# A chain of three transformer blocks on one core: four instead of three blocks of columns taken by halves of the tokens at a change of stage, their low parts made on DVE instead of POOL

## The chip, the core and the metric

The kernel runs on one core of a Trainium2 chip. The core has a matrix engine (PE, with its weight loads PEld), a vector engine (DVE), an activation engine (ACT), a general engine (POOL) and a queue engine that issues loads (SP). The metric is the time of one execution in microseconds on the device; lower is better.

## The reference

512 tokens of width 1024 go through three blocks, all in float32. What matters here is where a new activation meets its first weights:

```
x = layer_norm(DN_ALPHA * x + 0.5 * swiglu_ffn(x, ffn1_wg, ffn1_wu, ffn1_wd), ...)      # ffn1
y = parallel_mixers(x, w_in, ...)     # h @ w_in: qkv, z, gates, glu; gated delta rule, conv branch
x = layer_norm(DN_ALPHA * x + y, ...)
x = layer_norm(DN_ALPHA * x + memory_cross_attention(x, mem, w_xq, ...), ...)           # x @ w_xq
x = layer_norm(DN_ALPHA * x + 0.5 * swiglu_ffn(x, ffn2_wg, ffn2_wu, ffn2_wd), ...)      # ffn2
x = second_block(x, ...)              # retention and sparse attention
x = third_block(x, ...)               # neighbourhood and latent attention, then a SwiGLU (ffn3)
```

`swiglu_ffn` is `(silu(x @ w_gate) * (x @ w_up)) @ w_down`. In `parallel_mixers` the product with `w_in` gives, per head, the queries, keys and values of a chunked gated delta rule (GDN), the gates of its decay, and the two halves of a gated linear unit (GLU) for a 31-tap convolution.

## The kernel before

**Products.** A float32 product is made of three matmuls in a reduced type: every operand is split into a high part and a low part (`mm3`, lines 210 to 214). A weight block is loaded by `wload` (line 349): SP loads 128 x 1024 values to a raw buffer `wr` (2 buffers), ACT casts them to the high part `wh` (line 346; 4 buffers), and an engine that the caller names subtracts to get the low part `wl` (line 347; 4 buffers). That engine is DVE, except in the GDN stage (`now["lo"] = G`), and where the caller passes POOL (`G`).

**Changes of stage.** A stage ends in `block_out` (line 474): the last products of the four rows of 128 tokens are consumed one row after another. Each row goes through a chain on DVE: add the residual (line 493), statistics (509, 376), the reciprocal root (line 370, with a power on POOL, line 371), two instructions of line 381 and two of line 382, which scale and shift the two halves of the row. Each half is then turned by four PE transposes (line 364) and split on ACT and DVE (lines 346 and 347, `x<-mm`), which makes the new activation.

**By halves.** The next stage needs all four rows for a matmul over 512 tokens, but only rows one and two for one over the first 256. So at the start of ffn1, GDN, cross-attention, ffn2 and ffn3 the function `by_halves` (line 409) loads some blocks of 128 columns, takes all of them over the first half of the tokens, and then all of them over the second: 24 matmuls of 256 columns per block and half. Before, these are three blocks: gate, gate and up in the three ffn (a fourth block, the second up, follows over 512 tokens), key, query and value of head 0 in GDN, three blocks of queries in cross-attention. The low parts are made by POOL, except in ffn1's start, where three blocks were loaded early with DVE (`early`).

**What sets the order.** The code is written as generators; a scheduler places each engine's instructions in one order by its own estimate of times, within the dependences. Each engine runs its own order and waits where an operand is not there. In the GDN stage the order of emission is kept (`keep_order`): a list of units (24 matmuls of a block, line 294) fills PE between the steps of the chains (`procs`), and DVE is filled with convolution taps (line 654). There, the PSUM banks are shared out by `banks(pj=3, tp=1, gt=3, cv=1)`.

Of the kernel before, what the change touches and what calls it, by code (L numbers as in the profile page):

```python
# [108 lines left out]
def kernel(ctx: ExitStack, tc: tile.TileContext, a: dict, out: bass.AP, upto=99):  # L109
# [299 lines left out]
    def by_halves(jobs, act):  # L409


        ws = []
        for src, c0, banks in jobs:
            n = len(banks)
            ws.append(early.pop(0) if early else
                      [wload(src, k0, 8 // n, c0, n * 128, G) for k0 in range(0, 8, 8 // n)])
        for hf in range(2):
            ts_ = slice(hf * 256, (hf + 1) * 256)
            for (src, c0, banks), w in zip(jobs, ws):
                n = len(banks)  # L420
                for i in range(n):
                    cs = slice(i * 128, (i + 1) * 128)
                    for k in range(8):
                        h, l = w[k // (8 // n)]
                        mm3(banks[i][:, ts_], (h[:, k % (8 // n), cs], l[:, k % (8 // n), cs]),
                            (act.hi(k)[:, ts_], act.lo(k)[:, ts_]), k == 0, k == 7)
                yield
# [112 lines left out]
    def swiglu(act, wg, gc, wu, uc, scale, h, f0, f1, first=None):  # L540

        wg, wu = dram_w(wg), dram_w(wu)
        for fp in range(f0, f1, 2):
            ps = []
            if fp == f0 == first:
                ps = [[bank(), bank()], [bank(), bank()]]
                yield from by_halves([(w, c0 + (fp + f) * 128, [ps[i][f]])
                                      for i, f, w, c0 in ((0, 0, wg, gc), (0, 1, wg, gc), (1, 0, wu, uc))], act)
                wh, wl = wload(wu, 0, 8, uc + (fp + 1) * 128, 128)
                for k in range(8):  # L550
                    mm3(ps[1][1], (wh[:, k], wl[:, k]), (act.hi(k), act.lo(k)), k == 0, k == 7)
                yield
            for w, c0 in ((wg, gc), (wu, uc)) if not ps else ():
                pp = [bank(), bank()]
                ps.append(pp)
                for kh in range(2):
                    hi, lo = wload(w, 4 * kh, 4, c0 + fp * 128, 256)
                    for f in range(2):
                        cs = slice(f * 128, (f + 1) * 128)
                        for k in range(4):  # L560
                            mm3(pp[f], (hi[:, k, cs], lo[:, k, cs]), (act.hi(4 * kh + k), act.lo(4 * kh + k)),
                                kh == 0 and k == 0, kh == 1 and k == 3)
                    yield
            for f in range(2):
                sg = t2()
                A.activation(sg, ps[0][f], AF.Silu)  # L566
                V.scalar_tensor_tensor(sg, sg, scale, ps[1][f], OP.mult, OP.mult)  # L567
                split(sg, h.hi(fp + f), h.lo(fp + f), G)
            yield
# [65 lines left out]
    cv = {}  # L635

    def glu_conv(c):
        w = dram_w("w_in")
        act = acts["b1_1"]
        ps = []  # L640

        def taps(o):
            s_ = []

            def first():
                pad = work("pad", (128, T + 30))
                G.memset(pad[:, :30], 0.0)
                A.copy(pad[:, 30:], o)
                s_.extend((pad, bank(tag="cv")))
                A.activation(s_[1], pad[:, 0:T], AF.Identity, bias=cols["convb"][:, c:c + 1], scale=tap31(0, c))  # L650

            def tap(j):
                pad, p = s_
                V.scalar_tensor_tensor(p if j < 30 else o, pad[:, j:j + T], tap31(j, c), p, OP.mult, OP.add)  # L654

            background[1].append(first)
            background[1].extend([lambda j=j: tap(j) for j in range(1, 31)])

        def consume():
            if c % 2 == 0:  # L660
                cv.setdefault("out", []).append(slot(FT, tag="ma"))
            o = cv["out"][c // 2][:, c % 2]
            A.copy(o, ps[0])
            sg = work("xr", (128, T))
            A.activation(sg, ps[1], AF.Sigmoid)
            yield 1500.0
            G.tensor_tensor(o, o, sg, OP.mult)
            yield 1500.0
            taps(o)

        def body(h, l):
            p = bank()
            for k in range(8):
                mm3(p, (h[:, k], l[:, k]), (act.hi(k), act.lo(k)), k == 0, k == 7)
                yield 1
            ps.append(p)
            if len(ps) == 2:
                spawn(consume())

        unit((w, 0, 8, 4112 + c * 128, 128), body)  # L680
        unit((w, 0, 8, 4112 + 1024 + c * 128, 128), body)

    def conv_norm():
# [36 lines left out]
    gd = {}  # L720
# [79 lines left out]

    def gdn_start():
        ps = {i: bank() for i in (1, 0, 2)}
        gd["pre", 0] = ps
        yield from by_halves([(dram_w("w_in"), i * 1024, [ps[i]]) for i in (1, 0, 2)], acts["b1_1"])

    def gdn_rows(h):

# [411 lines left out]
    def cross_queries():  # L1219
        w = dram_w("w_xq")  # L1220
        act = acts["b1_2"]
        qt = xa["q"] = Act(slot)

        def consume(f, p):
            A.activation(qt.hi(f), p, AF.Copy, scale=1.0 / 16)
            V.scalar_tensor_tensor(qt.lo(f), p, 1.0 / 16, qt.hi(f).bitcast(FT), OP.mult, OP.subtract)

        ps = [bank() for _ in range(3)]
        yield from by_halves([(w, f * 128, [ps[f]]) for f in range(3)], act)
        for f in range(3):  # L1230
            consume(f, ps[f])
        yield from feature_proj(w, 384, 5, act, 8, lambda f, p: consume(f + 3, p))

    def cross_attention():
        qt = xa["q"]
# [761 lines left out]
    with ExitStack() as outer:  # L1997
        outer.enter_context(room(dict(ma=12)))
        mark("gdn")
        with room(vk=6, mt=4, at=4, Y=4, X=2, pad=2, xr=3, sq=1, t2=4, sqc=1, gsmall=1, ub=1, yb=1, tb=1):  # L2000
            sq, lev = t2((128, 3, 128)), work("sqc", (128, 2, 128))
            S.dma_start(sq, a["k_squares"][:, 1:4])
            for i, j in enumerate((2, 4)):
                S.dma_start(lev[:, i], a["k_squares"][:, j])
            triu, ones, gneg, lev = sq[:, 0], sq[:, 2], lev[:, 0], lev[:, 1:2]
            zero = work("sq", (128, 4, 128))
            V.memset(zero, 0.0)
            for t in ("sm", "sy", "sx"):
                gd[t] = dpool.tile([64, BLOCK_STEP], FT, name=t)
            for t in ("sy", "sx"):  # L2010
                for i in range(2):
                    S.dma_start(chunks(gd[t], i), zero)
            now["lo"] = G
            run(gdn_start())
            banks(pj=3, tp=1, gt=3, cv=1)
            gdn_rows(0)
            gdn_gates()
            spawn(gdn_pair(0))
            for what in (glu_conv, 0), (gdn_rows, 1), (glu_conv, 1), (gdn_rows, 2), (gdn_rows, 3), (glu_conv, 2), \
                    (gdn_rows, 4), (glu_conv, 3), (gdn_rows, 5), (gdn_z, 0), (gdn_z, 1), (glu_conv, 4), (gdn_rows, 6), \  # L2020
                    (gdn_rows, 7), (glu_conv, 5), (gdn_z, 2), (gdn_z, 3), (glu_conv, 6), (gdn_z, 4), (gdn_z, 5), \
                    (glu_conv, 7), (gdn_z, 6), (gdn_z, 7), *[(gdn_gate, f) for f in range(8)]:
                what[0](what[1])
            split_ahead(2)
            while True:
                fill_dve()
                start = len(nc.cur_bb.bb.instructions)
                if not step():
                    break
                keep_order(start)  # L2030
            for left in background[1]:
                left()
            now["lo"] = V
        wide()
        mark("mix2")
        with room(dict(m=10), mf=6, t2=5):
            run(gate_proj("gcx", "w_in", 7184, acts["b1_1"], None, "mf"))
            run(split_o())
            run(interleave((gated("ga", "w_gdn_out", gd["oact"], 8, None), 1.0), (seq(conv_norm(), conv_act()), 0.5)))
            run(merge("y1", "ga", "gcx", "w_conv_out", cv["act"], 8, cols["bco"], "ma"))  # L2040
            mark("mixout")
            run(block_out(acts["y1"], 8, dram_w("w_mix_out"), residual(x_dram["b1_1"], "mf"), ALPHA, ("ln2_g", "ln2_b"),
                          "b1_2", out if upto == 2 else None, tag="mf"))
# [126 lines left out]
```

## Time and profile before

| what | value |
|---|---|
| median of three runs | 2798.34 us (2793.07 to 2801.97) |
| profiled execution, its own time | 2799.25 us |
| its span, first to last instruction | 2797.5 us |
| mean granted clock of PE | 0.983 |
| PE busy | 2673.2 us (96%) |
| DVE busy | 1375.7 us (49%) |
| ACT busy | 1065.4 us (38%) |
| POOL busy | 477.5 us (17%) |

Busy shares are means over stages. PE's matmuls are pipelined, so that matmuls recorded with 0.28 us may follow each other every 0.12 us; the distance of their starts tells what one costs.

### The profile page before, as it was taken

How to read it: one execution, taken by the hardware profiler on the slowest of the kernel's cores; microseconds unless marked ns; L12 is line 12 of the kernel's file. 1: busy time of each engine (PE TensorE's matmuls, PEld its weight loads, DVE VectorE, ACT ScalarE, POOL GpSimd, SP SyncE). 2: the span in 40 equal slices, each digit the busy share in tenths (PEclk: the TensorE clock that was granted, in tenths of full speed). 3: DMA queues.
4: the chain of work that ended last, by engine and by line, in shares of the span. 5: the costliest groups of instructions: out<-in, count | busy, mean ns of one | idle time of the engine just before them, and what ended most of it. 6: DMA issues, size and time to landing. Idle time of an engine off the chain costs nothing. (4 is left out here: it accounts for less than half of the span.)

```text
span 2797.5 us, 34810 instructions
## 1 busy us (share of the span) xinstructions
PE 2673.2 (96%) x13600; PEld 2170.6 (78%) x13600; DVE 1375.7 (49%) x2459; ACT 1065.4 (38%) x2000; POOL 477.5 (17%) x357
## 2 busy tenths in 40 slices
PE   9999999897898899999999989999999999999998
PEld 7888877776677688888888867775786767888887
DVE  3232357665568556453332365674455464622324
ACT  3222236554543332433212254563255464332221
POOL 0101035343331011001101030131002001211011
PEclk9999999998999999999999999999999999999999
DMA  6323356556555234524333334312235122433332
GB/s 193 97 95 95 97 118 86 86 77 94 61 72 91 83 124 125 173 76 158 98 97 94 97 101 125 98 43 80 91 98 92 56 59 95 159 112 98 95 94 83
DMA packets 330421, 277.30 MB, mean 99 GB/s; under 512 B 50360, under 2 KB 282513, under 8 KB 330257
## 3 DMA queue, kind: packets, MB, share of 16 engines
q1 hardware_dynamic: 292768, 251.20, 35.3%
q10 hardware_dynamic: 37488, 23.88, 2.8%
q8 instruction: 107, 1.75, 0.3%
q14 instruction: 58, 0.47, 0.1%
HBM read 256.64 MB, written 20.49 MB: 99 GB/s over the span
## 5 line engine op out<-in xcount | busy, mean ns | idle before, releaser
L212 PE MATMUL mm<-x,wl 128*128 128x512 f32 (+3 forms) x2072 | 808.0, 390 | 8.9 <-POOL wl L347 5.9
L347 DVE TENSOR_TENSOR wl<-wr,wh 128x1024 fp32r<-128x1024 f32 (+1 forms) x351 | 429.4, 1224 | 784.5 <-ACT wh L346 783.3
L213 PE MATMUL mm<-x,wh 128*128 128x512 f32 (+3 forms) x2072 | 792.8, 383 | 0.0
L214 PE MATMUL mm<-x,wh 128*128 128x512 f32 (+3 forms) x2072 | 792.3, 382 | 0.0
L346 ACT CAST wh<-wr 128x1024 fp32r<-128x1024 f32 (+2 forms) x425 | 436.3, 1027 | 796.9 <-PE mm L214 523.9
L212 PEld LDWEIGHTS mm<-x,wl 128*128 128x128 f32 (+2 forms) x2072 | 395.1, 191 | 82.9 <-POOL wl L347 6.3
L214 PEld LDWEIGHTS mm<-x,wh 128*128 128x128 f32 (+2 forms) x2072 | 394.5, 190 | 75.9 <-issue 1.8
L213 PEld LDWEIGHTS mm<-x,wh 128*128 128x128 f32 (+2 forms) x2072 | 395.6, 191 | 68.4 <-issue 1.4
L347 POOL TENSOR_TENSOR wl<-wr,wh 128x1024 fp32r<-128x1024 f32 x74 | 177.0, 2394 | 543.9 <-ACT wh L346 521.6
L347 POOL TENSOR_TENSOR h<-t,h 128x512 fp32r<-128x512 f32 x66 | 101.6, 1539 | 837.0 <-ACT h L346 837.0
L214 PE MATMUL mm<-wh,h 128*128 128x512 f32 x528 | 205.6, 389 | 0.0
L212 PE MATMUL mm<-wh,h 128*128 128x512 f32 x528 | 205.6, 389 | 0.0
L213 PE MATMUL mm<-wl,h 128*128 128x512 f32 x528 | 205.6, 389 | 0.0
L654 DVE SCALAR_TENSOR_TENSOR mm<-pad,cols,mm 128x512 f32<-128x512 f32 x232 | 174.7, 753 | 27.4 <-ACT mm L650 21.8
L212 PEld LDWEIGHTS mm<-wh,h 128*128 128x128 f32 x528 | 99.1, 188 | 20.6
L214 PEld LDWEIGHTS mm<-wh,h 128*128 128x128 f32 x528 | 99.1, 188 | 20.5
L213 PEld LDWEIGHTS mm<-wl,h 128*128 128x128 f32 x528 | 99.1, 188 | 20.4
L566 ACT ACTIVATE t<-mm 128x512 f32<-128x512 f32 x66 | 39.4, 597 | 130.7 <-PE mm L214 130.7
L567 DVE SCALAR_TENSOR_TENSOR t<-t,mm 128x512 f32<-128x512 f32 x66 | 45.4, 687 | 78.1 <-POOL h L347 54.9
L212 PE MATMUL mm<-m,wl 128*128 128x512 f32 (+1 forms) x224 | 81.6, 364 | 0.0
L214 PE MATMUL mm<-m,wh 128*128 128x512 f32 (+1 forms) x224 | 81.3, 363 | 0.0
L213 PE MATMUL mm<-m,wh 128*128 128x512 f32 (+1 forms) x224 | 81.0, 362 | 0.0
(454 smaller groups left out, 3691.6 us busy)
## 6 DMA issues: line engine op xcount, KB each, us to landing
wr<-in_w_in SPq DMA_DIRECT2D x122, 512.0 KB
wr<-in_ffn_wg SPq DMA_DIRECT2D x44, 512.0 KB
wr<-in_ffn_wu SPq DMA_DIRECT2D x44, 512.0 KB
wr<-in_ffn_wd SPq DMA_DIRECT2D x44, 512.0 KB
wr<-in_w_ffn_in SPq DMA_DIRECT2D x44, 512.0 KB
wr<-in_w_ffn_out SPq DMA_DIRECT2D x22, 512.0 KB
xd<-m ACTq DMA_DIRECT2D x32, 256.0 KB
wr<-in_w_xkv SPq DMA_DIRECT2D x16, 512.0 KB
```

The lines of the kernel that those rows point to most:

```text
L212: PE.matmul(o, lh[1], rh[0], start=start, stop=False)
L213: PE.matmul(o, lh[0], rh[1], start=False, stop=False)
L214: PE.matmul(o, lh[0], rh[0], start=False, stop=stop)
L346: A.copy(hi, src)
L347: (eng or V).tensor_sub(lo, src, hi.bitcast(FT))
L566: A.activation(sg, ps[0][f], AF.Silu)
L567: V.scalar_tensor_tensor(sg, sg, scale, ps[1][f], OP.mult, OP.mult)
L654: V.scalar_tensor_tensor(p if j < 30 else o, pad[:, j:j + T], tap31(j, c), p, OP.mult, OP.add)
```

## The change

Four blocks go by halves instead of three. In the ffn stages the fourth is the second up block, which was taken over 512 tokens just behind. In cross-attention it is the fourth block of queries (of eight). In GDN it is the first block of the GLU's linear half, which was a unit of the stage before; its bank is taken from the tag `gt`, so that the banks are now shared out before `gdn_start` and not behind it, and `glu_conv(0)` finds that product ready. The low parts of all blocks that `by_halves` loads are made by DVE (`V`) instead of POOL (`G`).

```diff
@@ by_halves
             ws.append(early.pop(0) if early else
-                      [wload(src, k0, 8 // n, c0, n * 128, G) for k0 in range(0, 8, 8 // n)])
+                      [wload(src, k0, 8 // n, c0, n * 128, V) for k0 in range(0, 8, 8 // n)])
@@ swiglu
                 yield from by_halves([(w, c0 + (fp + f) * 128, [ps[i][f]])
-                                      for i, f, w, c0 in ((0, 0, wg, gc), (0, 1, wg, gc), (1, 0, wu, uc))], act)
-                wh, wl = wload(wu, 0, 8, uc + (fp + 1) * 128, 128)
-                for k in range(8):
-                    mm3(ps[1][1], (wh[:, k], wl[:, k]), (act.hi(k), act.lo(k)), k == 0, k == 7)
-                yield
+                                      for i, w, c0 in ((0, wg, gc), (1, wu, uc)) for f in range(2)], act)
@@ glu_conv
-        ps = []
+        ps = [gd["glu"]] if c == 0 else []
...
-        unit((w, 0, 8, 4112 + c * 128, 128), body)
+        if not ps:
+            unit((w, 0, 8, 4112 + c * 128, 128), body)
         unit((w, 0, 8, 4112 + 1024 + c * 128, 128), body)
@@ gdn_start
-        gd["pre", 0] = ps
-        yield from by_halves([(dram_w("w_in"), i * 1024, [ps[i]]) for i in (1, 0, 2)], acts["b1_1"])
+        gd["pre", 0], gd["glu"] = ps, bank(tag="gt")
+        yield from by_halves([(dram_w("w_in"), i * 1024, [ps[i]]) for i in (1, 0, 2)] +
+                             [(dram_w("w_in"), 4112, [gd["glu"]])], acts["b1_1"])
@@ cross_queries
-        ps = [bank() for _ in range(3)]
-        yield from by_halves([(w, f * 128, [ps[f]]) for f in range(3)], act)
-        for f in range(3):
+        ps = [bank() for _ in range(4)]
+        yield from by_halves([(w, f * 128, [ps[f]]) for f in range(4)], act)
+        for f in range(4):
             consume(f, ps[f])
-        yield from feature_proj(w, 384, 5, act, 8, lambda f, p: consume(f + 3, p))
+        yield from feature_proj(w, 512, 4, act, 8, lambda f, p: consume(f + 4, p))
@@ tile_decoder_kernel, the GDN stage
-            run(gdn_start())
             banks(pj=3, tp=1, gt=3, cv=1)
+            run(gdn_start())
```

DVE's order at the change from ffn1 to GDN, before, from the affine steps of the third row (`m_1098`) to the splits of the fourth row (`m_1100`):

```order
L381 SCALAR_TENSOR_TENSOR m_1098<-m_1098,mv_2527,m_2158 128x512 x2
L382 SCALAR_TENSOR_TENSOR m_1098<-m_1098,lr_2529,m_2160 128x512 x2
L493 SCALAR_TENSOR_TENSOR m_1100<-m_1100,mm_2331 128x512
L509 BN_STATS st_2326<-m_1100 128x6
L347 TENSOR_TENSOR x_2445<-mm_2535,x_2444 128x4x128
L376 BN_AGGR mv_2573<-st_2326 128x2
L347 TENSOR_TENSOR x_2457<-mm_2545,x_2456 128x4x128
L370 TENSOR_SCALAR lr_2575<-mv_2573 128x1
L381 SCALAR_TENSOR_TENSOR m_1100<-m_1100,mv_2573,m_2158 128x512 x2
L382 SCALAR_TENSOR_TENSOR m_1100<-m_1100,lr_2575,m_2160 128x512 x2
L347 TENSOR_TENSOR x_2445<-mm_2581,x_2444 128x4x128
L347 TENSOR_TENSOR x_2457<-mm_2591,x_2456 128x4x128
```

The same place after (the rows are `m_1122` and `m_1124` now):

```order
L382 SCALAR_TENSOR_TENSOR m_1122<-m_1122,lr_2553,m_2184 128x512 x2
L493 SCALAR_TENSOR_TENSOR m_1124<-m_1124,mm_2355 128x512
L347 TENSOR_TENSOR wl_2656<-wr_2654,wh_2655 128x1024
L347 TENSOR_TENSOR x_2469<-mm_2559,x_2468 128x4x128
L347 TENSOR_TENSOR x_2481<-mm_2569,x_2480 128x4x128
L509 BN_STATS st_2350<-m_1124 128x6
L347 TENSOR_TENSOR wl_2662<-wr_2660,wh_2661 128x1024
L376 BN_AGGR mv_2597<-st_2350 128x2
L370 TENSOR_SCALAR lr_2599<-mv_2597 128x1
L381 SCALAR_TENSOR_TENSOR m_1124<-m_1124,mv_2597,m_2182 128x512 x2
L382 SCALAR_TENSOR_TENSOR m_1124<-m_1124,lr_2599,m_2184 128x512 x2
L347 TENSOR_TENSOR wl_2668<-wr_2666,wh_2667 128x1024
```

The second, third and fourth blocks' subtractions (`wl`) now stand in DVE's order within the fourth row's chain; the first stands before line 493 of the first row. The other three changes of stage read alike, save that in them a fourth block's subtraction stood behind the last line 382 before, too.

PE's order at the same change of stage, before, where it meets the transposes of the fourth row (line 364), 43 half matmuls of 72 into the first half of the tokens:

```order
L214 MATMUL mm_2621<-x_2456,wh_2630 128x256
L212 MATMUL mm_2621<-x_2456,wl_2631 128x256
L364 MATMUL mm_2581<-ident,m_1100 128x128 x4
L213 MATMUL mm_2621<-x_2457,wh_2630 128x256
L214 MATMUL mm_2621<-x_2456,wh_2630 128x256
L364 MATMUL mm_2591<-ident,m_1100 128x128 x4
```

And after, 62 half matmuls of 96 into it:

```order
L212 MATMUL mm_2646<-x_2480,wl_2662 128x256
L213 MATMUL mm_2646<-x_2481,wh_2661 128x256
L364 MATMUL mm_2605<-ident,m_1124 128x128 x4
L214 MATMUL mm_2646<-x_2480,wh_2661 128x256
L212 MATMUL mm_2646<-x_2480,wl_2662 128x256
L364 MATMUL mm_2615<-ident,m_1124 128x128 x4
```

The transposes moved from the second block's first half (`mm_2621`) to the third's (`mm_2646`). Those of the third row stand after six and seven half matmuls in both.

## Rows read from the trace of the kernel before

**Rows 1.** Waits of PE: waiter, releaser, total us, times, longest.

```profile
PE mm L693 <- DVE ma L654: 12.3, 1, 12.3
...
PE mm L364 <- issue: 6.3, 4, 1.6
...
PE mm L364 <- DVE mf L382: 4.1, 2, 2.1
PE mm L364 <- DVE m L382: 4.1, 2, 2.1
```

**Rows 2.** Timeline, PE, into GDN: start, us, instruction, count, [idle before, releaser].

```profile
378.08 0.63 PE L364 MATMUL mm<-ident,m 128*128 128x128 f32 x4 [1.55 <-issue]
...
380.88 0.63 PE L364 MATMUL mm<-ident,m 128*128 128x128 f32 x4 [2.05 <-DVE m L382]
...
382.18 0.41 PE L212 MATMUL mm<-x,wl 128*128 128x256 f32 x1
382.39 0.41 PE L213 MATMUL mm<-x,wh 128*128 128x256 f32 x1
...
387.16 0.60 PE L364 MATMUL mm<-ident,m 128*128 128x128 f32 x4
387.51 0.36 PE L213 MATMUL mm<-x,wh 128*128 128x256 f32 x1
...
400.13 0.40 PE L212 MATMUL mm<-x,wl 128*16 128x512 f32 x1
```

**Rows 3.** Timeline, DVE, into GDN; the last row is from ffn2's start.

```profile
373.80 1.40 DVE L381 SCALAR_TENSOR_TENSOR m<-m,mv,m 128x512 f32<-128x512 f32 x2
375.12 5.62 DVE L382 SCALAR_TENSOR_TENSOR m<-m,lr,m 128x512 f32<-128x512 f32 x2
380.66 0.67 DVE L493 SCALAR_TENSOR_TENSOR m<-m,mm 128x512 f32<-128x512 f32 x1
...
384.62 1.41 DVE L382 SCALAR_TENSOR_TENSOR m<-m,lr,m 128x512 f32<-128x512 f32 x2
...
1268.65 1.22 DVE L347 TENSOR_TENSOR wl<-wr,wh 128x1024 fp32r<-128x1024 f32 x1
```

**Rows 4.** Timeline, POOL, into GDN.

```profile
373.96 0.98 POOL L371 TENSOR_TENSOR lr<-lr,nhalf 128x1 f32<-128x1 f32 x1 [4.30 <-DVE lr L370]
374.92 5.27 POOL L347 TENSOR_TENSOR wl<-wr,wh 128x1024 fp32r<-128x1024 f32 x2
```

**Rows 5.** Windows, PE: stretch, us, busy (count), granted clock, DMA share, GB/s.

```profile
375.66:400.13 24.47, 20.87 (x161) 0.93 0.64 149
1078.95:1106.01 27.06, 22.72 (x176) 0.94 0.51 157
1258.30:1283.80 25.50, 21.82 (x162) 0.87 0.65 222
2421.63:2445.88 24.25, 20.61 (x161) 0.93 0.69 233
```

**Rows 6.** Timeline, PE, ffn1: 24 half matmuls apart, then 24 full ones apart.

```profile
16.20 0.28 PE L214 MATMUL mm<-x,wh 128*128 128x256 f32 x1
...
19.08 0.28 PE L214 MATMUL mm<-x,wh 128*128 128x256 f32 x1
...
31.67 0.39 PE L213 MATMUL mm<-x,wh 128*128 128x512 f32 x1
...
37.12 0.39 PE L213 MATMUL mm<-x,wh 128*128 128x512 f32 x1
```

**Rows 7.** Timeline, ACT: a cast into GDN, and a fourth block's into ffn2.

```profile
374.55 1.06 ACT L346 CAST wh<-wr 128x1024 fp32r<-128x1024 f32 x1 [0.33 <-PE mm L214]
...
1265.20 1.05 ACT L346 CAST wh<-wr 128x1024 fp32r<-128x1024 f32 x1
```

**Rows 8.** Timeline, PE, GDN: the first joins of two pairs of heads.

```profile
506.12 1.16 PE L208 MATMUL mm<-X,mt 128*128 128x128 f32 x8 [1.32 <-DMA X<-sx]
...
580.59 2.11 PE L208 MATMUL mm<-X,mt 128*128 128x128 f32 x16 [1.42 <-DMA X<-sx]
```

**Rows 9.** Timeline, PE, cross-attention: transposes of the memory's second half.

```profile
1099.96 1.06 PE L1165 MATMUL mm<-ident,mf 128*128 128x128 f32 x8 [0.76 <-DMA mf<-in_mem]
```

More of the change, by code (lines that the diff above doesn't have):

```diff
@@ L2013 @@
             now["lo"] = G
+            banks(pj=3, tp=1, gt=3, cv=1)
             run(gdn_start())
-            banks(pj=3, tp=1, gt=3, cv=1)
             gdn_rows(0)
```

## The prediction

> **What bounds the kernel now.** I read the page first: PE is busy 96% of the span of 2797.5 us and every other engine half or less, so the time is PE's work plus the places where PE stands still. The view of who waited for whom, for PE, comes next [rows 1]. Its longest entry is one wait of 12.3 us on the vector engine, late in the GDN stage. For this change three other entries count: the transposes at line 364, by which a new activation enters a stage, waited 4 times on "issue" (6.3 us) and 4 times on the affine step of line 382 (4.1 + 4.1 us). That is twice at each of four changes of stage: into GDN, cross-attention, ffn2 and ffn3.
>
> The timeline of the first of them shows how [rows 2 to 4]. PE begins the half-token blocks at 375.66 us [rows 5]. After six matmuls it meets the two transposes of the third row of 128 tokens, and stands 1.55 and then 2.05 us, until 380.88. DVE is why: its two affine steps of that row, 1.41 us together for the fourth row at 384.62, take 5.62 us from 375.12 on [rows 3]. In just that time, from 374.92 for 5.27 us, POOL makes the low parts of two weight blocks [rows 4]; POOL's tiny power at 373.96 had not slowed the step at 373.80. So a large POOL subtraction holds back a DVE instruction that reads two SBUF tensors. After the two gaps PE's matmuls of 256 columns come 0.21 us apart (382.18 to 382.39) where they otherwise come 0.12 apart [rows 2, 6]; the granted clock of the four stretches is 0.87 to 0.94 [rows 5]. The gaps thus cost twice, as idle time and as matmuls at the 1.2 GHz level.
>
> **What the four places lose.** A block of 24 half matmuls takes 2.88 us (16.20 to 19.08), a group of four transposes adds 0.36 (387.16 to 387.51) [rows 2, 6]. Three blocks by two halves and the four groups of rows three and four then need 144 x 0.12 + 4 x 0.36 = 18.72 us. They take 24.47 (GDN), 25.50 (ffn2) and 24.25 (ffn3) [rows 5]: losses of 5.75, 6.78 and 5.53. Cross-attention has four more groups, of the memory's rows, so 20.16 of 27.18 (27.06 and the last matmul's own 0.12); less the 0.76 that these wait for their own load [rows 9] it loses 6.26.
>
> **The change part by part.** *DVE instead of POOL.* Per place three subtractions of some 2.6 us (two in 5.27) leave POOL and three of 1.22 (row at 1268.65 [rows 3]) join DVE, in its order: the first ahead of row one's chain, where DVE is idle and at GDN at worst 0.1 us late; the second behind the fourth row's first step (line 493); the third before its statistics are joined; the fourth block's, which was DVE's already except in GDN, behind its affine steps. With nothing from POOL beside them the third row's affine steps end at 376.5. PE gets to its transposes at 375.66 + 6 x 0.12 = 376.4, needs one half at that time (ready 375.9) and the other at 376.9: no wait. So both gaps go, and with them the slow clock.
>
> *What is late next.* Row four. Its chain on DVE ran from 380.66 to the end of line 382 at 386.03, 5.37 us. It now starts at 376.5 and has two subtractions in it: 376.5 + 5.4 + 2 x 1.2 = 384.3. The fourth block's subtraction ends at 385.5, the splits of the fourth row at 386.8. PE meets row four's transposes after 62 half matmuls of 96 (before: after 43 of 72), so at 375.66 + 62 x 0.12 + 2 x 0.36 = 383.8 for the first, whose half is ready at 383.6, and 384.4 for the second, ready at 384.3. That is a tie. The second block is needed at 379.3 (ready 378.3), the third at 382.2 (381.4), the fourth at 386.4 (385.5), the second half of the tokens at 389.1 (386.8). The casts that these subtractions wait for ran at 374.55 and, for a fourth block, at 1265.20, some 7 us into its place [rows 7]. Nothing waits by more than some tenths. *Four blocks* is what keeps it so: with three, row four's transposes would stand at 375.66 + 43 x 0.12 + 0.72 = 381.5, 2.8 us before their data.
>
> *Price of halves.* The fourth block took 24 matmuls of 512 columns, 5.45 us (31.67 to 37.12), and takes 2 x 2.88 [rows 6]: 0.31 more, at five places (ffn1's start too, where three low parts were DVE's already; its fourth load now stands among the small column loads on SP, some 1.5 us for those, which PE's column transposes have in hand).
>
> *Cross-attention.* The load of the memory's second half waits on SP for the write of row four, and PE waited 0.76 us for it [rows 9]. The write moves up by some 3 us and PE gets there some 3.5 sooner, so I put 0.5 against the gain.
>
> *GDN.* There the fourth block was not the next work: it is the first GLU block, and 5.45 us of PE filler leave the stage that follows. That stage is a chain: gates, decay, scores, a solve by way of DRAM, joins. PE waits for its loads at the joins (1.32 us at 506.12, 1.42 at 580.59 [rows 8]), so filler taken out before a join is partly paid back as a longer wait. The gates begin at 400.13 before [rows 2] and at 375.66 + 192 x 0.12 + 1.44 = 400.1 after: the chain starts no sooner. By the order 318 full matmuls instead of 336 stand between gates and first join, and 147 instead of 156 before the last scores: these come 9 x 0.227 = 2.0 us sooner, and the solve with them. From the second join on the order is as before, to the 12.3 us wait at the end, which keeps its taps. Bounds: 0 (the chain ignores PE) and 5.75 - 0.31 = 5.4 (PE's gain passes whole). I take 2.0, the scores' move.
>
> **A rule weighed.** Rows 3 and 4 show a POOL operation holding a DVE one. The Trainium skill, page "SBUF — State Buffer", section "SBUF: two separate sides", says that the two share a port pair as an exclusive lock, for a DVE operation with two SBUF inputs against a GpSimd one that reads SBUF, and that whichever starts first keeps it for its whole length. By that the new subtractions on DVE could in turn hold POOL's power step of the row's norm (line 371). The rows show that power running beside line 381, at 373.96, unharmed, and in the new order no subtraction stands between line 370 and line 382. By the rule it costs nothing here, unless the engines drift by a subtraction, which is rival two's price.
>
> **Sum.** GDN 2.0; cross-attention 6.26 - 0.31 - 0.5 = 5.4; ffn2 6.78 - 0.31 = 6.5; ffn3 5.53 - 0.31 = 5.2; ffn1 -0.3. Together 18.8. The profiled run took 2799.25 us (span 2797.5), 0.9 above the median of 2798.34, which is nothing. 2799.25 - 18.8 = 2780.5.
>
> **The rivals.** *One, GDN takes it back.* Filler leaves ahead of the first join and DVE, ACT and POOL orders shift up to the second; if the solve doesn't come sooner and a queue adds a wait like those of rows 8 at one or two joins, GDN ends 0 to 4 us later: 2780.5 + 2 + 0 to 4, about 2784 to 2787. For it: PE does wait at both joins. Against: the scores move up.
>
> *Two, DVE becomes late.* Row four is a tie, so if DVE's three subtractions cost one instruction more (1.2 us) PE stands at the transposes again, 1.2 us at each of four places, 4.9 together: 2785. If the gap also drops the clock, which it did behind gaps of 1.6 and 2.1 us and then cost about 1.7 (19 matmuls 0.09 us too far apart), 11.7: 2792. For it: no slack in the sum above. Against: two tenths of slack at the next steps, and a gap under those seen.
>
> *Three, slower than before.* DVE works in order, and the second subtraction stands ahead of both splits of the third row and of row four's statistics. Its cast (374.55, done 375.6) waits for a buffer that PE's last matmuls of the old stage free, and its raw weights for a load. If one came late, DVE's whole chain would stand behind it and PE behind the chain. To eat the gain at the three places outside GDN (17 us) and GDN's 2 it must be 4.7 us late at each place, so not before 381.8. The cast is 1.5 us ahead of its need: it decides only from 6 us later on; 2803 at 6 us.
>
> *Four, all of it passes.* GDN's 5.4 and no memory wait: 22.7, so 2776.5.
>
> **How the numbers follow.** Forecast with rival four (2774 to 2784): 0.66. Rival one 0.14, rival two 0.16, rival three 0.04. The range holds the forecast with the spread of the three runs (some 4 us either way) below rival four, and reaches up over rival one and the dearer part of rival two's first price: 2773 to 2791. About 0.3%, 8.4 us, is what a measurement of this kernel can tell from none: faster means below some 2790. All of the forecast, of rival one and half of rival two lie there, less a little for the spread: faster 0.85, same 0.11, slower 0.04.
>
> **What would show it.** Line 382 in no place above 0.8 us an instruction; no PE wait at line 364 but a few tenths; granted clock 1.0 in the four stretches; POOL without large subtractions there. Per place PE needs 192 x 0.12 + 1.44 = 24.5 us for four blocks (26 in cross-attention). In GDN the first join at about 504 us, with a PE wait of 2 to 4 us before it, and its end some 2 us sooner. Wrong it would be by a new wait at row four's transposes, by a low clock without a gap, or by a GDN stage that is longer than before.

## The result, and the profile after

The changed kernel takes 2774.56 us (median of four runs, 2771.17 to 2778.54) where the kernel before takes 2795.70 (four runs, 2792.01 to 2801.97). The ratio is 0.9923, 95% interval 0.9911 to 0.9935: 21.5 us less, between 18.2 and 24.9. Forecast were 2780.5 us, 18.8 less than the profiled run of before.

PE's waits in the changed kernel (waiter, releaser, total us, times, longest) no longer hold the three entries at line 364 on "issue" (a wait for which the profile shows no releaser) and on line 382 that [rows 1] show. One of 2.5 us on a low part of weights is new:

```profile
PE mm L690 <- DVE ma L650: 13.4, 1, 13.4
...
PE mm L364 <- DMA m<-in_x: 5.8, 2, 5.0
...
PE mm L212 <- DVE wl L347: 2.5, 1, 2.5
```

The stretches of [rows 5], now four blocks by two halves each, PE alone (stretch, us, busy, granted clock, DMA share, GB/s):

```profile
377.01:404.51 27.50, 25.02 (x209) 1.00 0.67 153
1071.47:1098.13 26.66, 26.66 (x225) 1.00 0.53 178
1244.73:1269.51 24.78, 24.78 (x210) 1.00 0.79 271
2401.51:2426.27 24.76, 24.76 (x209) 1.00 0.79 274
```

In three of the four PE is busy for the whole stretch, and the granted clock is 1.00 in all, where it was 0.87 to 0.94. DVE's timeline at GDN's start (start, us, instruction) answers to [rows 3]:

```profile
376.48 1.41 DVE L382 SCALAR_TENSOR_TENSOR m<-m,lr,m 128x512 f32<-128x512 f32 x2
...
378.41 1.22 DVE L347 TENSOR_TENSOR wl<-wr,wh 128x1024 fp32r<-128x1024 f32 x1
...
384.10 1.41 DVE L382 SCALAR_TENSOR_TENSOR m<-m,lr,m 128x512 f32<-128x512 f32 x2
388.75 1.23 DVE L347 TENSOR_TENSOR wl<-wr,wh 128x1024 fp32r<-128x1024 f32 x1 [3.24 <-ACT wh L346]
```

The third row's two steps of line 382 take 1.41 us where they took 5.62. The last row is the fourth block's low part, which DVE makes 3.24 us late. Behind it stand the cast and the load (ACT, then SP), and PE waits for it:

```profile
387.67 1.04 ACT L346 CAST wh<-wr 128x1024 fp32r<-128x1024 f32 x1 [8.16 <-DMA wr<-in_w_in]
```

```profile
379.65 0.37 SPq L353 DMA_DIRECT2D wr<-in_w_in  x1
```

```profile
390.03 0.38 PE L212 MATMUL mm<-x,wl 128*128 128x256 f32 x1 [2.48 <-DVE wl L347]
```

The load is issued at 379.65, just when the second block's subtraction (378.41, 1.22 us) is done: there are two raw buffers, and that subtraction frees the one that the fourth block needs. The data are there 8.0 us later.

Both traces by stretches, each from its first half-token matmul to the next one's:

| stretch | before | after | less | forecast |
|---|---|---|---|---|
| start, ffn1 | 375.66 | 377.01 | -1.35 | -0.3 |
| GDN to cross-attention | 703.29 | 694.46 | 8.83 | 2.0 |
| cross-attention to ffn2 | 179.35 | 173.26 | 6.09 | 5.4 |
| ffn2 to ffn3 | 1163.33 | 1156.78 | 6.55 | 6.5 |
| ffn3 to the end | 375.87 | 370.89 | 4.98 | 5.2 |
| span | 2797.5 | 2772.4 | 25.1 | 18.8 |

These two executions lie 25.1 us apart, the runs 21.5.

### The profile page after: what moved, and what is told of

It is laid out like the page before. It is cut to its first block, busy times and chain, and to the rows that moved or that the text cites. A ratio compares the mean times of both kernels' runs of the same rounds, so it can differ in the third digit from the quotient of the medians.

```text
span 2772.4 us, 35041 instructions
## 1 busy us (share of the span) xinstructions
PE 2670.9 (96%) x13720; PEld 2173.4 (78%) x13720; DVE 1370.9 (49%) x2472; ACT 1064.5 (38%) x1999; POOL 445.2 (16%) x344
## 5 line engine op out<-in xcount | busy, mean ns | idle before, releaser
L347 DVE TENSOR_TENSOR wl<-wr,wh 128x1024 fp32r<-128x1024 f32 (+3 forms) x364 | 444.5, 1221 | 801.1 <-ACT wh L346 799.7
L212 PE MATMUL mm<-x,wl 128*128 128x512 f32 (+1 forms) x2112 | 812.9, 385 | 10.7 <-POOL wl L347 5.9
L214 PE MATMUL mm<-x,wh 128*128 128x512 f32 (+1 forms) x2112 | 797.9, 378 | 0.0
L213 PE MATMUL mm<-x,wh 128*128 128x512 f32 (+1 forms) x2112 | 797.8, 378 | 0.0
L346 ACT CAST wh<-wr 128x1024 fp32r<-128x1024 f32 (+3 forms) x425 | 436.3, 1027 | 811.0 <-PE mm L214 502.7
L212 PEld LDWEIGHTS mm<-x,wl 128*128 128x128 f32 x2112 | 400.4, 190 | 83.1 <-POOL wl L347 6.3
L214 PEld LDWEIGHTS mm<-x,wh 128*128 128x128 f32 x2112 | 400.1, 189 | 74.3 <-issue 1.8
L213 PEld LDWEIGHTS mm<-x,wh 128*128 128x128 f32 x2112 | 401.0, 190 | 67.2 <-issue 1.4
L347 POOL TENSOR_TENSOR wl<-wr,wh 128x1024 fp32r<-128x1024 f32 (+1 forms) x61 | 144.2, 2364 | 297.3 <-ACT wh L346 279.1
L371 POOL TENSOR_TENSOR lr<-lr,nhalf 128x1 f32<-128x1 f32 x24 | 23.6, 984 | 371.3 <-DVE lr L370 371.3
L214 PE MATMUL mm<-m,wh 128*128 128x512 f32 (+1 forms) x224 | 81.2, 363 | 0.0
```

Of the source, the lines that this page charges most:

```text
L212: PE.matmul(o, lh[1], rh[0], start=start, stop=False)
L213: PE.matmul(o, lh[0], rh[1], start=False, stop=False)
L214: PE.matmul(o, lh[0], rh[0], start=False, stop=stop)
L346: A.copy(hi, src)
L347: (eng or V).tensor_sub(lo, src, hi.bitcast(FT))
L371: G.tensor_tensor(o, o, nhalf[:, :n], OP.pow)
```

## The experiments

Three questions: is it the engine or the fourth block that gains; what holds DVE while POOL works; and what is GDN's share, 2.0 or 8.8 us.

**e1: the engine alone.** Three blocks as before, low parts on DVE.

```diff
-                      [wload(src, k0, 8 // n, c0, n * 128, G) for k0 in range(0, 8, 8 // n)])
+                      [wload(src, k0, 8 // n, c0, n * 128, V) for k0 in range(0, 8, 8 // n)])
```

> The kernel before with one edit: the low parts in by_halves are made by DVE, the blocks stay three. Theory A (the prediction's: the fourth block is the cover that row four needs): each of the four changes of stage gains the third row's 5 to 6 us and loses 2.8 us at the transposes of row four, so about 11 us of the changed kernel's gain are missing: ratio to before 0.9955 to 0.997, PE waits of 2 to 3 us at line 364 four times. Theory B (DVE alone makes the gain, the fourth block is nearly free of effect): in PE's order of this kernel the transposes of row four already stand after 62 half matmuls, of 72, as they do in the changed kernel, of 96. In the changed kernel they were met at 385.31 and 386.00 us without a wait, and 72 half matmuls would end at 387.3; with three blocks PE then needs row four's splits, which the changed kernel's DVE could have done about 1.4 us behind the second transposes, so a wait of 0 to 1.5 us at each of four places, against 0.31 saved at five places: ratio 0.991 to 0.9935, no wait at line 364 above 0.5 us.

Ratio 0.9931 (0.9919 to 0.9944), median 2778.09 against 2798.15: 19.3 us less, 15.7 to 22.7, the changed kernel's gain within the intervals. Theory B holds. Its stretches on PE, three blocks each:

```profile
376.56:397.30 20.74, 19.23 (x162) 1.00 0.61 141
1072.62:1093.52 20.90, 20.90 (x178) 1.00 0.64 203
1246.49:1265.51 19.02, 19.02 (x161) 1.00 0.77 262
2404.45:2423.46 19.01, 19.01 (x162) 1.00 0.74 255
```

The last three have no idle time, and the 19.02 and 19.01 us of the ffn stand beside the prediction's 18.72. Outside GDN row four is not late without the fourth block. Its transposes stand after 62 half matmuls in PE's order here too, and after 43 again in e2, which has four blocks: it is the move to DVE that shifts them, not the fourth block. GDN's start alone has a wait, of 1.51 us; e7 takes that up.

**e2: the fourth block alone.** The changed kernel with POOL for the low parts again.

```diff
-                      [wload(src, k0, 8 // n, c0, n * 128, V) for k0 in range(0, 8, 8 // n)])
+                      [wload(src, k0, 8 // n, c0, n * 128, G) for k0 in range(0, 8, 8 // n)])
```

> The changed kernel with one edit: POOL makes the low parts in by_halves again, the blocks stay four. Theory A (POOL's subtractions hold DVE's line 382, whatever the number of blocks): line 382 of the third row takes 5 us and more for its two halves, PE waits 1.5 and 2 us at line 364 four times, the granted clock of these stretches stays at 0.87 to 0.95; the time is that of before, or up to 4 us above it (five times 0.31 us for the halves, and some half microsecond in ffn1): ratio 1.000 to 1.002. Theory B (more half-token work is what hides the late row, whoever subtracts): most of the gain stays, ratio 0.992 to 0.995.

Ratio 0.9998 (0.9989 to 1.0007): theory A, nothing is gained. At ffn2's start, DVE and then POOL:

```profile
1255.91 5.62 DVE L382 SCALAR_TENSOR_TENSOR mf<-mf,lr,mf 128x512 f32<-128x512 f32 x2
```

```profile
1255.71 5.27 POOL L347 TENSOR_TENSOR wl<-wr,wh 128x1024 fp32r<-128x1024 f32 x2
```

The same 5.62 and 5.27 as in [rows 3, 4], and PE waits 1.57 and 2.05 us there again:

```profile
1258.87 0.63 PE L364 MATMUL mm<-ident,mf 128*128 128x128 f32 x4 [1.57 <-issue]
...
1261.67 0.63 PE L364 MATMUL mm<-ident,mf 128*128 128x128 f32 x4 [2.05 <-DVE mf L382]
```

**e3: POOL's subtraction in four pieces.** The kernel before, with

```diff
+        A.copy(hi[:, :n], raw[:, :n])
+        for i in range(0, n, n // cuts):
+            cs = slice(i, i + n // cuts)
+            (eng or now["lo"]).tensor_sub(lo[:, cs], raw[:, cs], hi[:, cs].bitcast(FT))
```

in place of `split`, and `cuts=4` from `by_halves`.

> The kernel before with one edit: each subtraction of by_halves on POOL is cut into four of 256 columns, some 0.65 to 0.75 us each. Theory A (a POOL subtraction keeps DVE's two-input instruction out for the whole of the one that is running, and lets it in between two): line 382 of the third row, two instructions, takes 1.4 plus at most two pieces, 2.2 to 3 us instead of 5.62; PE's two waits of 1.55 and 2.05 fall to about 1 us together at each of four places and the clock stays up: ratio 0.994 to 0.9965. Theory B (the two engines share a rate while both work): the two take as long together however POOL's work is cut, line 382 stays at 5 us and more: ratio 0.999 to 1.002. Theory C (POOL has its next piece ready and goes first each time): line 382 comes when POOL is done, as in B.

Ratio 0.9974 (0.9965 to 0.9983), so 7.3 us less. Line 382 (385 here) takes 2.37 us for its two steps, as theory A has it, and theories B and C are out. DVE, then POOL, at ffn2's start:

```profile
1253.55 2.37 DVE L385 SCALAR_TENSOR_TENSOR mf<-mf,lr,mf 128x512 f32<-128x512 f32 x2
...
1261.51 1.41 DVE L385 SCALAR_TENSOR_TENSOR mf<-mf,lr,mf 128x512 f32<-128x512 f32 x2 [1.14 <-POOL lr L374]
```

```profile
1253.35 7.62 POOL L357 TENSOR_TENSOR wl<-wr,wh 128x256 fp32r<-128x256 f32 x8
1260.93 0.55 POOL L374 TENSOR_TENSOR lr<-lr,nhalf 128x1 f32<-128x1 f32 x1
```

The gain is smaller than I had put it because a second wait takes over: eight pieces last 7.62 us where two whole ones lasted 5.27, the power of row four's norm stands behind them in POOL's order, DVE waits 1.14 us for it, and PE 1.35 us at row four's transposes (3.54 at GDN's start, where the power also stands behind the gates' small subtraction, as in e1 below). The pieces are not slow in themselves. Looked at one at a time, three of the eight start 0.70 us apart; those beside DVE's steps of lines 384 and 385 (381 and 382 before) take longer, up to 1.25 us, so here POOL seems to wait for DVE as well:

```profile
1255.33 1.18 POOL L357 TENSOR_TENSOR wl<-wr,wh 128x256 fp32r<-128x256 f32 x1
...
1257.17 0.73 POOL L357 TENSOR_TENSOR wl<-wr,wh 128x256 fp32r<-128x256 f32 x1
```

In the kernel before, looked at one instruction at a time, DVE and then POOL:

```profile
375.12 2.86 DVE L382 SCALAR_TENSOR_TENSOR m<-m,lr,m 128x512 f32<-128x512 f32 x1
...
377.90 2.83 DVE L382 SCALAR_TENSOR_TENSOR m<-m,lr,m 128x512 f32<-128x512 f32 x1
```

```profile
374.92 2.51 POOL L347 TENSOR_TENSOR wl<-wr,wh 128x1024 fp32r<-128x1024 f32 x1
...
377.40 2.79 POOL L347 TENSOR_TENSOR wl<-wr,wh 128x1024 fp32r<-128x1024 f32 x1
```

Each step of DVE ends 0.5 us behind one subtraction of POOL (377.98 and 377.43; 380.73 and 380.19): it stands until that one is done, and is let in before the next. The waiting is inside the 2.86 us of its record and not shown as idle time. This is what the rule quoted in the prediction says (the Trainium skill, page "SBUF — State Buffer", section "SBUF: two separate sides"): an exclusive lock for the length of one instruction. The trace agrees; a shared rate (theory B) would have left e3's 2.37 at 5 us and more.

**e8: one operand instead of two on POOL.** The kernel before, POOL copying the high part instead of subtracting, so that the low part itself is left out.

```diff
+            A.copy(hi[:, :n], raw[:, :n])
+            G.tensor_copy(lo[:, :n], hi[:, :n].bitcast(FT))
```

> The kernel before, with POOL's subtraction in by_halves replaced by a POOL copy of the high part to the low part's tile (the low part itself is left out): one SBUF operand instead of two, everything else in the same order. Theory A (any POOL instruction of this size that reads SBUF keeps DVE's two-input instruction out until it ends): line 382 of the third row lasts as long as POOL's two copies, PE waits at line 364 as before or a little shorter, if the copy is a little shorter than the subtraction's 2.5 us: ratio 0.997 to 1.001. Theory B (only a POOL instruction with two SBUF operands does so): line 382 takes 1.4 us for its two, the waits at the third row are gone, and what is left is row four, as in e3 with its waits of 1.4 us: ratio 0.991 to 0.996.

Ratio 0.9938 (0.9921 to 0.9955), in theory B's range, but the mechanism is theory A's. ffn2's start, DVE and POOL:

```profile
1245.83 2.97 DVE L386 SCALAR_TENSOR_TENSOR mf<-mf,lr,mf 128x512 f32<-128x512 f32 x2
```

```profile
1245.61 2.65 POOL L356 CAST wl<-wh 128x1024 fp32r<-128x1024 f32 x2
```

The two steps last as long as POOL's two copies again; only, these are twice as short, and PE's waits fall to 0.29 and 0.74 us. I had a copy "a little shorter" than a subtraction, which made the ratio unfit to tell the theories apart; the rows do.

**e4, e7: GDN's start with three blocks.** e4 is the changed kernel with the GLU block as a unit again.

```diff
-        ps = [gd["glu"]] if c == 0 else []
+        ps = []
...
-        yield from by_halves([(dram_w("w_in"), i * 1024, [ps[i]]) for i in (1, 0, 2)] +
-                             [(dram_w("w_in"), 4112, [gd["glu"]])], acts["b1_1"])
+        yield from by_halves([(dram_w("w_in"), i * 1024, [ps[i]]) for i in (1, 0, 2)], acts["b1_1"])
```

> The changed kernel with the GDN start taken back to three blocks (key, query, value; low parts still by DVE), the first GLU block being a unit of the stage again. The GDN stage, from its first half matmul to cross-attention's, took 703.3 us before and 694.5 in the changed kernel, 8.8 less, where 2.0 had been forecast. Theory A (taking the GLU block out of the chain gives the surplus): the stage is at 698 to 702 us here, ratio to before 0.9935 to 0.996. Theory B (DVE's low parts give it all, and the chain passes on what PE gains): the wait of 2.48 us for the fourth block's low part goes, a wait of up to 1.5 us for row four's splits may come, the stage stays at 692 to 696 us, ratio 0.991 to 0.993.

Ratio 0.9930 (0.9916 to 0.9944); the stage takes 692.9 us, theory B. The wait for row four is 2.09 us here, more than B allowed. In e1 it reads, on DVE and POOL:

```profile
385.68 1.42 DVE L382 SCALAR_TENSOR_TENSOR m<-m,lr,m 128x512 f32<-128x512 f32 x2 [1.94 <-POOL lr L371]
```

```profile
384.68 0.45 POOL L347 TENSOR_TENSOR wl<-wr,wh 128x128 fp32r<-128x128 f32 x1 [8.81 <-ACT wh L346]
385.09 0.55 POOL L371 TENSOR_TENSOR lr<-lr,nhalf 128x1 f32<-128x1 f32 x1
```

POOL's power for row four stands behind the gates' small subtraction, and that behind its load. e7 is e1 with these two exchanged in POOL's order, and nothing else moved on any engine:

```diff
         (eng or V).tensor_sub(lo, src, hi.bitcast(FT))
+        if eng is G and list(src.shape) == [128, 128] and "gates" not in now:
+            now["gates"] = True
+            tc.add_manual_dep(nc.cur_bb.bb.instructions[-1], now["pow"].name, mybir.DependencyInfo(
+                mybir.DependencyClass.NoSync, mybir.DependencyReason.DATA), reason="behind the power")
...
         G.tensor_tensor(o, o, nhalf[:, :n], OP.pow)
+        now["pow"] = nc.cur_bb.bb.instructions[-1]
```

> Three blocks by halves with low parts on DVE (as in e1), and in GDN one instruction moved: POOL's subtraction for the gates' small block, which stood in POOL's order ahead of the power of row four's norm and waited there for a load, now stands behind it. If that queue made the wait of 1.5 us (2.1 in e4) at row four's transposes, the wait falls to 0.3 us or less, line 382 of row four follows line 381 within 0.2 us on DVE, and the time is 1 to 2 us below e1's: ratio 0.990 to 0.9925. If the wait has another cause it stays, ratio as in e1, 0.993.

The wait is gone, the GDN start takes what the ffn take, all at full clock:

```profile
375.53:394.54 19.01, 19.01 (x162) 1.00 0.68 157
```

Ratio 0.9922 (0.9905 to 0.9939). That is the changed kernel's 0.9923 and, within the intervals, e1's 0.9931: 1.5 us do not show in the runs, only in the trace.

**e5, e6, e10, e11: GDN's share.** e5 makes the change in GDN's start alone; e10 and e11 are the same program again, e6 is the kernel before again.

```diff
+        yield from by_halves([(dram_w("w_in"), i * 1024, [ps[i]]) for i in (1, 0, 2)] +
+                             [(dram_w("w_in"), 4112, [gd["glu"]])], acts["b1_1"], V)
...
-                      [wload(src, k0, 8 // n, c0, n * 128, G) for k0 in range(0, 8, 8 // n)])
+                      [wload(src, k0, 8 // n, c0, n * 128, lo or G) for k0 in range(0, 8, 8 // n)])
```

> The kernel before with the change at one place alone: GDN's start takes four blocks by halves, their low parts on DVE; the other four uses of by_halves stay as they were. By the prediction's sum this is worth 2.0 us (2.4 at the place itself with the new wait of 2.48 us for the fourth block): ratio 0.999 to 0.9995. By the two traces the GDN stage lost 8.8 us: if this belongs to the change, ratio 0.9965 to 0.998 and a GDN stage of 693 to 697 us from its first half matmul to cross-attention's; if 3 to 5 us of it were that one execution of before, ratio 0.9975 to 0.999 and the stage of the kernel before, looked at once more, comes out shorter than 703.

> The kernel before, unchanged, looked at once more. If the length of the GDN stage (703.3 us in the trace of before; 692.9 to 700.2 in the five kernels with other starts) varies between executions of one program, the stretch from the second join at 580.59 to the one at 690.13, 109.5 us there and 104.5 to 107.6 in the others though its order is the same in all, comes out at 104 to 108 here; if not, at 109 to 110.

> The kernel of e5 (the change in GDN's start alone), looked at once more. Its twelve executions lay in two groups, five from 2791.3 to 2795.5 us and seven from 2799.9 to 2802.7, and the trace of e5 is one of the first group. If this one is of the second, the stretch that is longer by some 6 us is to be found by comparing it with e5's: within GDN, in the chain that goes by way of DRAM, or in the second block, whose order is the same in both.

> As e10, once more: the same program, so that there is a trace of either group with a better chance; the same two places are looked at.

e5's ratio is 0.9999 (0.9988 to 1.0010): the place is worth between 3.4 us less and 2.8 more. So the whole kernel gained at most 3.4 of the 8.8 us by which the two traces differ in this stage. The GDN stage on PE, in e5, e10, e11 (one program) and in e6:

```profile
375.62:1068.26 692.64, 628.48 (x3411) 0.95 0.52 90
```

```profile
376.58:1079.09 702.51, 638.33 (x3410) 0.94 0.51 89
```

```profile
375.69:1072.27 696.58, 633.07 (x3410) 0.95 0.51 90
```

```profile
375.64:1082.02 706.38, 638.28 (x3386) 0.94 0.51 89
```

One program takes from 692.6 to 702.5 us for this stage, with the same matmuls. e10's longer time is PE's busy time (9.9 us more): the same matmuls took longer, at a lower granted clock (0.94 against 0.95 over 700 us, to the two digits shown). In one stretch, from 684.08 to 787.83 in e5 and from 689.46 to 798.39 in e10, 4.1 of the 5.2 us between them are PE's busy time, and the clock is 0.91 and 0.88:

```profile
684.08:787.83 103.75, 91.63 (x527) 75.78 (x528) 57.49 (x126) 49.76 (x113) 39.12 (x27) 0.91 0.55 80
```

```profile
689.46:798.39 108.93, 95.69 (x527) 78.59 (x528) 57.65 (x126) 49.61 (x114) 39.62 (x27) 0.88 0.53 77
```

(Here the columns are PE, PEld, DVE, ACT and POOL, each busy time with its count, ahead of the clock.) e6's stretch between the joins, which I expected at 104 to 108 or at 109 to 110, is 108.7 (584.14 to 692.80), between the two. Summed over each trace's records of the granted clock, the stage stands at the 1.2 GHz level for 68 us in e5, 75 in e11 and 82 in e10, in the order of its length. What sets the clock in this stage differently from one execution to the next, these runs do not tell.

One thing speaks against reading e5's ratio as this stage's gain alone. In all three of its traces the stage is shorter than in both of the kernel before (703.3 and 706.4), but from its end to the end of the span they take 1724.1, 1721.6 and 1723.3 us (e5, e10, e11), where the kernel before takes 1718.6 and 1718.1 with as many matmuls there. Why the rest is longer was not tested.

**e9: all of GDN's low parts on DVE.** e7, and `now["lo"] = V` for the GDN stage. The exchange of e7 has no effect in it, since the gates' subtraction is DVE's too; PE waits 1.94 us at row four's transposes again.

```diff
-            now["lo"] = G
+            now["lo"] = V
```

> The kernel of e7 (three blocks, low parts on DVE, POOL's power ahead of the gates' subtraction) with all other low parts of the GDN stage on DVE too, some 52 subtractions that POOL made in 2.39 us each. If the hold seen at the changes of stage also costs time in this stage's chains, PE's waits there on POOL (5.9 us for a low part, 8.1 for line 1073) go and the ratio is 0.987 to 0.991; if DVE, which ends the stage with convolution taps that PE waits 12 us for, becomes later by the 52 x 1.22 = 63 us that it takes over, less the taps' idle time, that wait grows and the ratio is 0.995 or more.

Ratio 1.0069 (1.0052 to 1.0087) to the kernel before, where e7 has 0.9922. PE's waits at the stage's end:

```profile
PE mm L698 <- DVE ma L659: 59.2, 3, 24.2
```

DVE is busy 493.6 us in the stage instead of 445.7 in e7, its convolution taps come later, and PE waits 59.2 us on them instead of 12.0. Here, where DVE ends the stage, POOL's slower subtraction is the better one.

## Why the prediction was right, and where it was not

- **The mechanism held.** Line 382 is at 0.7 us a step in all four places, the waits at line 364 are gone, the clock is 1.00. e2 and e3 show that it is POOL's subtraction, and its length, that held DVE.
- **The power was not "unharmed".** At 373.96, beside line 381, it took 0.98 us, and it takes 0.55 where DVE stands idle (385.09 in e1). So DVE seems to hold POOL too, as in e3's pieces. It cost nothing, as the prediction says, since line 381 itself lasts 1.4 us.
- **The three places outside GDN** were forecast at 5.4, 6.5 and 5.2 us and came to 6.09, 6.55 and 4.98 in the traces, 17.6 for 17.1. In cross-attention no wait for the memory's load came, for which 0.5 had been taken off.
- **The tie at row four** came out as worked: PE met its transposes 8.30 us after the first half matmul (385.31; forecast 8.1), and the second half of line 382 ended 8.5 after it (forecast 8.6). Each stood without a recorded wait.
- **"Four blocks is what keeps it so" was wrong.** It took the 43 half matmuls of the old order for what three blocks would have with the new engine. e1's order has 62, and no wait outside GDN. So the price of halves, 5 x 0.31 us, bought nothing that the runs show: 0.9931 without and 0.9923 with the fourth block.
- **The fourth low part in GDN was timed by its cast, not by its load.** "The fourth at 386.4 (ready 385.5)" left out that the raw buffer is freed by the second block's subtraction, which had moved from POOL into row four's chain on DVE, and that the load takes 8.0 us. It was ready at 389.98, 12.97 us after the first half matmul instead of 9.8, and PE waited 2.48 (1.70 to 3.72 in e5, e10 and e11). In ffn2 the load was issued as long after the first half matmul, 2.64 us (1247.37), and the subtraction ended 9.6 after it, as worked out: only the load was quicker, 3.8 us to its cast (1251.21; in cross-attention 4.2, from 1074.07 to 1078.24). The time of need was off as well: by the prediction's own terms it is 375.66 + 72 x 0.12 + 4 x 0.36 = 385.7, not 386.4 (and 388.6, not 389.1, for the second half). PE came to it 10.5 us after the first half matmul, between the two.
- **ffn1** lost 1.35 instead of 0.3. Of it 0.65 is seven matmuls at the start 0.21 apart instead of 0.12, before the clock rises; the three kernels with four blocks there begin GDN's blocks at 377.0 to 378.0, the traces with three at 375.5 to 377.2.
- **GDN's term, 2.0**, was neither shown nor refuted: e5 gives 0.3 less, from 3.4 less to 2.8 more. With 16.3 us from the other stretches of the traces it makes 16.6, and with e5's upper end 19.7; the runs say 18.2 to 24.9. So nothing contradicts the sum, but whether more than 3.4 us came from GDN in the changed kernel stays open; execution by execution this stage varies by 10 us, and one pair of traces cannot carry such a term. That the first join came at 503.93, as forecast (about 504), is luck: the gates began at 404.51 and not at 400.1, and from there to the join it was 99.4 us, where it was 106.0 before and forecast were 104. The wait before it was 0.60 us and not 2 to 4.
- **The rivals.** "DVE becomes late" and "GDN takes it back" did not come (the latter's price, 2780.5 + 2 + 0 to 4, is 2782.5 to 2786.5, not 2784 to 2787). Rival four's 2776.5 lies nearer to the measured 2774.56 than the forecast does, but of its two parts only the half microsecond in cross-attention is shown; its 5.4 for GDN lies outside e5's interval. The third, a queue held by a late load, came in a small form: 2.48 us on DVE in GDN, and in e1 and e4 on POOL, where I had not looked for it.

## What to carry to other kernels

A vector instruction that is longer than its like elsewhere may be waiting inside its own record: put the POOL instructions of the same time beside it before looking for a dependence. Move work off POOL where PE waits for a short DVE chain, and leave it on POOL where DVE itself ends the stage (e9). When a change moves an engine and adds cover at once, try the engine alone first: here it was all of the gain that the runs can tell (0.9931 and 0.9923).

## What was unexpected of the hardware

- DVE is let in between two queued POOL instructions: pieces of 256 columns brought two steps from 5.62 to 2.37 us, though POOL's next piece was ready. Four pieces alone took 2.82 us (from 1236.98 in e3), little more than the 2.51 of a whole subtraction; beside DVE's two-operand steps one piece takes up to 1.25.
- A POOL copy with one SBUF operand holds DVE's two-operand step as a subtraction does (2.97 us for two steps beside 2.65 of copies).
- A gap does not always cost the clock: after 2.48 us in the changed kernel the matmuls were 0.12 us apart again from the third one on, at a granted clock of 1.00 for the stretch, while e5's 1.98 us went with 0.94 in its stretch.
- Fourth loads of 128 x 1024 values took 8.0 us from issue to cast from `w_in`, 4.2 from `w_xq` and 3.8 from ffn2's `wu`. Other transfers ran beside them; no run here separates the matrix from these.
